# A recurrent branch with its first tap, two squares and small copies on ScalarE, and gelu's polynomial in one VectorE operation

## The chip, the cores and the metric

The kernel runs on one core of a Trainium2 chip. A core has a matmul engine (TensorE, PE in the profile), VectorE (DVE), ScalarE (ACT), GpSimd (POOL) and a sync engine that issues DMAs (SyncE, SP). Each engine works through its own instructions in order; semaphores make one engine wait for another. The metric is device microseconds of the whole program, the median of several runs.

## The reference

One layer of a hybrid decoder for 2048 tokens of width 1024, all in float32:

```python
h = rms_norm(x, g1)
z = h @ w_in                                   # q, k, v, xr, gr
attn = dilated_attention(q, k, v)              # 8 heads, three dilations
xr = causal_depthwise_conv(xr, conv_w, conv_b) # 4 taps in time
r = sigmoid(xr @ w_r + b_r); i = sigmoid(xr @ w_i + b_i)
a = exp(-8 * r * softplus(-lam))
u = sqrt(1 - a * a) * (i * xr)
hid[t] = a[t] * hid[t - 1] + u[t]
rec = hid * gelu(gr)
x = x + rms_norm(concat(attn, rec) @ w_out, g2)
x = x + rms_norm(squared_relu_mlp(rms_norm(x, g3), w1, w2), g4)
```

What the change touches lies between `xr` and `rec`: the recurrent branch.

## The kernel before

The tokens are worked in two halves of 1024, each in two token blocks of 512, and the 512 channels of the recurrent branch in four groups of 128. So the branch consists of 16 blocks of 128 channels by 512 tokens; a block is named half_group_token block, so 1_2_0 is the first token block of group 2 in the second half. `recurrent_block` (L296 to L345) computes one.

Every matrix product with weights is made in three matmuls of a high and a low part: the weights are split on arrival by `split` (L54 on ACT, L55 on POOL or DVE), and `product` (L198 to L200) adds the three up over eight steps of the inner dimension in one PSUM bank.

A block runs as follows. `product` gives the conv input. DVE puts the last three inputs of the token block before it ahead of the new ones (L303, from `tail`), scales the product by the tokens' norm into `xr` (L304), and keeps the new last three (L305). POOL makes the first tap (L307), DVE adds three more (L310), all in `xc`. PE makes the two gates' products from `xc`, `pr` (L313) and `pi` (L315), which outside the kernel's start share a PSUM bank with one buffer. ACT turns them into `r` (L318) and `i` (L320) by tanh, then makes `th` (L323) and, in place of `r`, the factor a by exp (L324). DVE squares a (L326, named `a2`) and takes it into `th` (L327), ACT takes the root (L328), DVE multiplies (L329, L330), runs the recurrence over the 512 tokens (L331, the scan) into `xc`, and keeps its last value in `state` (L332). A second product goes through DVE as `gr` (L335); its gelu is a polynomial on POOL (L338 to L340), a tanh on ACT (L341) and two DVE steps (L342, L343). The block is then written to DRAM by a DMA that POOL issues (L345).

`xr`, `r`, `i`, `th`, `a2`, `gr` and `ge` have one buffer each, so a block's tile waits for the last reader of the block before it. The functions of ACT come in tables; a change of table is a row ACT_TABLE_LOAD.

The blocks are strung together with the attention: `ORDER` (L1557) interleaves the first half's recurrent groups (r02, r03), its products of q, k, v and two attention parts; `BETWEEN` holds the four groups of the second half; groups 0 and 1 of the first half come before both. Up to about 600 us the order on each engine is the scheduler's: it plays the program through a timeline of its own (`schedule_with_timeline_sim`) and issues each instruction where that timeline has it ready. So a change of an instruction's engine moves others. From the out-projection on, the order of the rest is fixed elsewhere.

`cst["pool"]` is an instruction behind which POOL issues copies of w_out and w2 to DRAM scratch (L1459), eight DMAs behind each group of the second half.

## Time and profile before

| | us |
|---|---|
| median of three runs | 2313.2 (2310.83 to 2317.4) |
| the profiled execution | 2311.64 |
| its span in the trace | 2309.9 |

| engine | busy us | share of the span |
|---|---|---|
| PE | 2184.8 | 95% |
| DVE | 1539.9 | 67% |
| ACT | 1231.3 | 53% |
| POOL | 465.9 | 20% |

Of the chain of work that ended last, PE is 59%, DVE 14%, DMA 9% and ACT 7%. The shares are means over a program whose stages differ: in the first 600 us attention, the recurrent branch and the input products share the engines, and from there on the out-projection and the MLP run. What a step of the recurrent branch costs must be read where it runs, as the idle time of PE in front of an instruction and as the clock PE is granted there (1.00 stands for full speed).

### The profile page before, as it was taken

Reading aid. Unit: us, or ns where it says so; the run is one execution under the profiler, and the core shown is the slowest. Engines: PE = TensorE matmul, PEld = TensorE weight load, DVE = VectorE, ACT = ScalarE, POOL = GpSimd, SP = SyncE. Lnnn points to the kernel's source line nnn. Section 1 sums busy time; section 2 is a strip of 40 time slices with the busy share of each in tenths; the row PEclk is TensorE's granted clock in tenths of the full one; section 3 lists DMA queues with packets and bytes.
Section 4 is the critical chain, followed back from the end, with each engine's and each line's share of the span. In section 5 each row is a group of like instructions: output and inputs, shape, how many; then the busy total and the mean of one; then the engine's idle time right before and its main releaser. Section 6 shows DMA issues by size and latency. Waiting matters only on the chain.

```text
span 2309.9 us, 30833 instructions
## 1 busy us (share of the span) xinstructions
PE 2184.8 (95%) x10264; PEld 1776.1 (77%) x10264; DVE 1539.9 (67%) x3060; ACT 1231.3 (53%) x2489; POOL 465.9 (20%) x549
## 2 busy tenths in 40 slices
PE   8989989889999899998999999889999999999998
PEld 6668778667788677786777787667878888788887
DVE  6757575887548877674667677767775656545556
ACT  7646464645334555453656666745454545563542
POOL 5543514563213201011001011113200000000003
PEclk9999999999999999999999999999999999999999
DMA  8364574645754586867777777768454433576665
GB/s 288 99 194 154 166 232 146 180 144 151 255 166 155 195 306 255 302 232 268 248 201 211 220 227 204 220 189 257 147 194 169 164 137 155 208 271 195 192 192 182
DMA packets 217553, 466.16 MB, mean 202 GB/s; under 512 B 22465, under 2 KB 77153, under 8 KB 211121
## 3 DMA queue, kind: packets, MB, share of 16 engines
q1 hardware_dynamic: 188624, 329.52, 45.7%
q0 software_dynamic: 28768, 134.66, 16.5%
q8 instruction: 81, 1.33, 0.2%
q14 instruction: 80, 0.65, 0.1%
HBM read 329.75 MB, written 151.13 MB: 208 GB/s over the span
## 4 chain that ended last, share of the span: by engine, by line
PE 59%; DVE 14%; DMA 9%; ACT 7%; issue 5%; POOL 1%; SPq 0%; DVEq 0%; ACTq 0%; POOLq 0%
PE o L1141 6%; PE o L1140 6%; PE o L1142 6%; PE za L1001 4%; PE za L1002 4%; PE za L1003 4%; PE z L198 3%; PE z L199 3%; PE z L200 3%; PE m L827 2%; PE m L825 2%; PE m L826 2%; PE zc L1001 2%; PE zc L1002 2%; PE zc L1003 2%
## 5 line engine op out<-in xcount | busy, mean ns | idle before, releaser
L198 PE MATMUL z<-hH,wH 128*128 128x512 f32 x640 | 263.6, 412 | 17.6 <-ACT wH L54 7.9
L199 PE MATMUL z<-hL,wH 128*128 128x512 f32 x640 | 259.1, 405 | 0.5 <-DVE hL L173 0.5
L200 PE MATMUL z<-hH,wL 128*128 128x512 f32 x640 | 257.9, 404 | 0.0
L198 PEld LDWEIGHTS z<-hH,wH 128*128 128x128 f32 x640 | 122.6, 192 | 51.2 <-ACT wH L54 8.8
L199 PEld LDWEIGHTS z<-hL,wH 128*128 128x128 f32 x640 | 122.3, 191 | 32.0 <-issue 5.1
L200 PEld LDWEIGHTS z<-hH,wL 128*128 128x128 f32 x640 | 122.5, 191 | 28.5 <-issue 3.4
L415 ACT ACTIVATE smB<-smB,negB 128x128 f32<-128x128 f32 (+3 forms) x128 | 71.4, 559 | 103.0 <-DVE negB L411 102.7
L55 POOL TENSOR_TENSOR wL<-wraw,wH 128x512 fp32r<-128x512 f32 x58 | 84.2, 1464 | 115.7 <-ACT wH L54 109.0
L1006 ACT ACTIVATE sq<-sq 128x512 f32<-128x512 f32 x93 | 58.8, 632 | 84.9 <-DVE sq L1010 84.9
L1066 POOL DMA_DIRECT2D sa<-sq x31 | 16.5, 533 | 402.4 <-ACT sq L1007 401.8
L415 ACT ACTIVATE sm<-sm,neg 128x256 f32<-128x256 f32 (+1 forms) x128 | 63.1, 494 | 55.7 <-DVE neg L411 55.2
L55 DVE TENSOR_TENSOR tlB<-pT_B,thB 128x384 fp32r<-128x384 f32 x96 | 57.4, 598 | 44.2 <-ACT thB L54 41.0
L1007 ACT ACTIVATE sq<-sq 128x512 f32<-128x512 f32 x124 | 76.6, 629 | 2.2
L54 ACT CAST wH<-wraw 128x512 fp32r<-128x512 f32 (+1 forms) x81 | 47.2, 612 | 49.5 <-PE z L199 31.7
L1174 POOL TENSOR_TENSOR y<-y,g4b 128x512 f32<-128x512 f32 x8 | 13.0, 1655 | 261.3 <-ACT junk_y L84 261.3
L1077 DVE TENSOR_TENSOR w2s<-w2s 128x512 f32<-128x512 f32 x64 | 44.1, 689 | 32.1 <-DMA w2s<-in_dram 31.2
L404 DVE CUSTOM_DVE_ANT_0 smB<-SB,mask_b 128x128 f32<-128x128 f32 (+3 forms) x128 | 59.5, 482 | 6.8 <-PE pT_B L377 4.2
L377 PE MATMUL pT_B<-ident,smB 128*128 128x128 f32 x320 | 52.7, 280 | 5.3 <-DVE nb L398 2.2
L54 ACT CAST thB<-pT_B 128x384 fp32r<-128x384 f32 x96 | 48.4, 506 | 16.3 <-PE oB L612 14.2
L55 DVE TENSOR_TENSOR tlA<-pT,thA 128x512 fp32r<-128x512 f32 (+1 forms) x64 | 42.5, 668 | 21.0 <-ACT thA L54 20.7
L1001 PE MATMUL za<-hHT,f_6H 128*128 128x512 f32 x128 | 50.6, 396 | 5.2 <-ACT sq L1040 5.1
L1002 PE MATMUL za<-hLT,f_5H 128*128 128x512 f32 x128 | 51.0, 399 | 4.4 <-DVE hLT L55 4.4
(568 smaller groups left out, 7105.7 us busy)
## 6 DMA issues: line engine op xcount, KB each, us to landing
sa<-as POOLq DMA_DIRECT2D x32, 1024.0 KB, 6.5
w1r<-in_dram SPq DMA_DIRECT2D x58, 512.0 KB, 3.8
sa<-sq POOLq DMA_DIRECT2D x31, 768.0 KB, 3.9
wraw<-in_dram SPq DMA_DIRECT2D x79, 256.0 KB, 3.5
w2s<-in_dram SPq DMA_DIRECT2D x16, 1024.0 KB, 7.5
sb<-w2s POOLq DMA_DIRECT2D x16, 1024.0 KB, 6.2
kh<-sk SPq DMA_DIRECT2D x24, 512.0 KB, 5.2
kl<-sk SPq DMA_DIRECT2D x24, 512.0 KB, 6.8
```

The costliest lines, as they stand in the source:

```text
L54: return (nc.scalar.copy(out=hi, in_=src), (lo_eng or nc.vector).tensor_tensor(out=lo, in0=src, in1=f32(hi), op=ALU.subtract))
L55: (lo_eng or nc.vector).tensor_tensor(out=lo, in0=src, in1=f32(hi), op=ALU.subtract))
L198: pe.matmul(z, hi[:, k, :], hh, start=(k == 0), stop=False)
L199: pe.matmul(z, hi[:, k, :], hl, start=False, stop=False)
L200: pe.matmul(z, lo[:, k, :], hh, start=False, stop=(k == KT - 1))
L415: s.activation(out=sm[:, c0:c0 + w], in_=sm[:, c0:c0 + w], func=AF.Exp, bias=neg[:, j:j + 1], accum_out=st[:, 1, u, cols[j]:cols[j] + 1])
L1001: pe.matmul(o, hi[:, k], bh[:, k], start=start and k == 0, stop=False, skip_group_check=True)
L1002: pe.matmul(o, hi[:, k], bl[:, k], start=False, stop=False, skip_group_check=True)
L1003: pe.matmul(o, lo[:, k], bh[:, k], start=False, stop=k == KH - 1, skip_group_check=True)
L1140: pe.matmul(o, ah[:, ts], bh, start=fresh and j == 0, stop=False, skip_group_check=True)
L1141: pe.matmul(o, ah[:, ts], bl, start=False, stop=False, skip_group_check=True)
L1142: pe.matmul(o, al[:, ts], bh, start=False, stop=j == NJ - 1, skip_group_check=True)
```

## The change

Four edits in `recurrent_block`, and one that follows from them:

- the two small copies (L303, L305) go from DVE to ACT;
- the first tap goes from POOL to ACT, as an activation with the tap's weight as scale and the bias as bias;
- a's square goes from DVE to ACT;
- gelu's square goes from POOL to ACT, and the two POOL steps behind it become one DVE step, (gr²+1/0.044715)·gr; the constant 0.044715 moves into the scale of the tanh;
- since the first tap is no longer on POOL, `cst["pool"]` becomes POOL's last weight split in `load_w`.

```diff
--- before.py
+++ after.py
@@ -108,7 +108,9 @@
             k0 = half * (KT // 2)
             raw = (px or self.pa).tile([P, KT // 2, P], F32, tag="wraw", bufs=6 if px else 2, name=f"wraw{hf}_{ct}_{half}")
             nc.sync.dma_start(out=raw, in_=self.w_in[ct, :, k0:k0 + KT // 2, :])
-            split(nc, hi[:, k0:k0 + KT // 2, :], lo[:, k0:k0 + KT // 2, :], raw, lo_eng=lo_eng or self.lo)
+            made = split(nc, hi[:, k0:k0 + KT // 2, :], lo[:, k0:k0 + KT // 2, :], raw, lo_eng=lo_eng or self.lo)
+            if not px and self.lo is nc.gpsimd:
+                self.cst["pool"] = made[1]
         return hi, lo
 
     def load_start(self, ct, px):
@@ -295,17 +297,16 @@
 
     def recurrent_block(self, hf, c, b, wx, wg, px):
         nc, p, vec = self.nc, px if px and c % 2 else self.pl, self.vec
-        v, s, g, pe = nc.vector, nc.scalar, nc.gpsimd, nc.tensor
+        v, s, pe = nc.vector, nc.scalar, nc.tensor
         n = f"{hf}_{c}_{b}"
         t0 = hf * HT + b * TB
         zx = self.product(hf, 12 + c, wx, b, "B" if px else "P")
         xr = p.tile([P, TB + 3], F32, tag="xr", bufs=1, name=f"xr{n}")
-        v.tensor_copy(out=xr[:, 0:3], in_=self.tail[:, c, :])
+        s.copy(out=xr[:, 0:3], in_=self.tail[:, c, :])
         v.tensor_tensor(out=in_time(xr[:, 3:TB + 3]), in0=by_residue(zx), in1=by_residue(self.bc[b]), op=ALU.mult)
-        v.tensor_copy(out=self.tail[:, c, :], in_=xr[:, TB:TB + 3])
+        s.copy(out=self.tail[:, c, :], in_=xr[:, TB:TB + 3])
         xc = p.tile([P, TB], F32, tag="xc", bufs=2 if p is self.pl else 1, name=f"xc{n}")
-        self.cst["pool"] = g.tensor_scalar(out=xc, in0=xr[:, 3:TB + 3], scalar1=self.cw[:, c, 3:4],
-                                           scalar2=vec["cb"][:, c:c + 1], op0=ALU.mult, op1=ALU.add)
+        s.activation(out=xc, in_=xr[:, 3:TB + 3], func=AF.Identity, scale=self.cw[:, c, 3:4], bias=vec["cb"][:, c:c + 1])
         for t in (2, 1, 0):
             v.scalar_tensor_tensor(out=xc, in0=xr[:, t:t + TB], scalar=self.cw[:, c, t:t + 1], in1=xc,
                                    op0=ALU.mult, op1=ALU.add)
@@ -323,7 +324,7 @@
         s.activation(out=th, in_=r, func=AF.Tanh, scale=self.pcs[:, c:c + 1], bias=self.pcs[:, c:c + 1])
         s.activation(out=r, in_=r, func=AF.Exp, scale=self.ncs[:, c:c + 1], bias=self.ncs[:, c:c + 1])
         a2 = p.tile([P, TB], F32, tag="la", bufs=1, name=f"a2{n}")
-        v.tensor_tensor(out=a2, in0=r, in1=r, op=ALU.mult)
+        s.activation(out=a2, in_=r, func=AF.Square)
         v.scalar_tensor_tensor(out=th, in0=a2, scalar=1.0, in1=th, op0=ALU.add, op1=ALU.mult)
         s.activation(out=th, in_=th, func=AF.Sqrt, scale=0.25)
         v.scalar_tensor_tensor(out=i, in0=i, scalar=1.0, in1=xc, op0=ALU.add, op1=ALU.mult)
@@ -335,10 +336,9 @@
         v.tensor_tensor(out=gr, in0=zg, in1=self.bc[b], op=ALU.mult)
 
         ge = p.tile([P, TB], F32, tag="ge", bufs=1, name=f"ge{n}")
-        g.tensor_tensor(out=ge, in0=gr, in1=gr, op=ALU.mult)
-        g.tensor_scalar(out=ge, in0=ge, scalar1=0.044715, scalar2=1.0, op0=ALU.mult, op1=ALU.add)
-        g.tensor_tensor(out=ge, in0=ge, in1=gr, op=ALU.mult)
-        s.activation(out=ge, in_=ge, func=AF.Tanh, scale=SQ2PI)
+        s.activation(out=ge, in_=gr, func=AF.Square)
+        v.scalar_tensor_tensor(out=ge, in0=ge, scalar=1.0 / 0.044715, in1=gr, op0=ALU.add, op1=ALU.mult)
+        s.activation(out=ge, in_=ge, func=AF.Tanh, scale=SQ2PI * 0.044715)
         v.scalar_tensor_tensor(out=ge, in0=ge, scalar=1.0, in1=gr, op0=ALU.add, op1=ALU.mult)
         v.scalar_tensor_tensor(out=by_residue(ge), in0=by_residue(ge), scalar=0.5, in1=in_time(xc), op0=ALU.mult,
                                op1=ALU.mult)
```

Lines of the new kernel stand a little lower: L303 becomes L305, L304 L306, L305 L307, the first tap L309, the taps L311, `pr` L314, `pi` L316, `r` L319, `i` L321, `th` L324, a by exp L325, a's square L327, its use L328, the root L329, L329 to L332 become L330 to L333, `gr` L336, gelu's square L339, its polynomial L340; L341 to L345 keep their numbers, and L198 to L200 become L200 to L202.

The order on PE before, around `pr` and `pi` of block 1_2_1, with products of z1_15_0 (conv input of block 1_3_0) at both sides:

```order
L199 MATMUL z1_15_0_5289<-hL2_3_3314,wH1_15_5269 128x512
L200 MATMUL z1_15_0_5289<-hH2_3_3313,wL1_15_5270 128x512
L198 MATMUL z1_15_0_5289<-hH2_4_3319,wH1_15_5269 128x512
L199 MATMUL z1_15_0_5289<-hL2_4_3320,wH1_15_5269 128x512
L313 MATMUL pr1_2_1_5207<-xc1_2_1_5202,bd_r_232 128x512
L315 MATMUL pi1_2_1_5209<-xc1_2_1_5202,bd_i_236 128x512
L200 MATMUL z1_15_0_5289<-hH2_4_3319,wL1_15_5270 128x512
L198 MATMUL z1_15_0_5289<-hH2_5_3325,wH1_15_5269 128x512
```

`pi` follows `pr` at once and writes the same bank.

On PE now, the rows around the same `pr`, with attention's output (oB) ahead of it:

```order
L612 MATMUL oB0_6_0_4303<-tlB0_4321,vb0_6_4170 128x256
L612 MATMUL oB0_6_0_4303<-thB0_4320,vb0_6_4170 128x128
L612 MATMUL oB0_6_0_4303<-tlB0_4321,vb0_6_4170 128x128
L314 MATMUL pr1_2_1_5194<-xc1_2_1_5189,bd_r_232 128x512
L202 MATMUL z1_15_0_5275<-hH2_5_3317,wL1_15_5256 128x512
L200 MATMUL z1_15_0_5275<-hH2_6_3323,wH1_15_5255 128x512
L201 MATMUL z1_15_0_5275<-hL2_6_3324,wH1_15_5255 128x512
```

`pr` is followed by the products of z1_15_0, and `pi` comes 30 rows later.

On PE now, the rows around `pi` of that block, with attention (oB, the transposed scores pT) ahead and a product of group 3's gate (z1_19_0) behind:

```order
L612 MATMUL oB0_6_2_4355<-thB0_4372,vb0_6_4170 128x128
L612 MATMUL oB0_6_2_4355<-tlB0_4373,vb0_6_4170 128x128
L377 MATMUL pT0_0_7_0_1_4430<-ident_60,sm0_7_2_4419 128x128 x2
L316 MATMUL pi1_2_1_5196<-xc1_2_1_5189,bd_i_236 128x512
L202 MATMUL z1_19_0_5328<-hH2_3_3305,wL1_19_5266 128x512
L200 MATMUL z1_19_0_5328<-hH2_4_3311,wH1_19_5265 128x512
```

`pr` and `pi` stood back to back; now 29 rows of PE stand between them.

The order on ACT before, in the same place, from r of block 1_2_0 to r of 1_2_1:

```order
L318 ACTIVATE r1_2_0_5123<-pr1_2_0_5119,vec_br_226 128x512
L323 ACTIVATE th1_2_0_5127<-r1_2_0_5123,pcs_271 128x512
L324 ACTIVATE r1_2_0_5123<-r1_2_0_5123,ncs_270 128x512
L328 ACT_TABLE_LOAD
L328 ACTIVATE th1_2_0_5127<-th1_2_0_5127 128x512
L54 CAST wH1_19_5279<-wraw1_19_0_5281 128x512
L320 ACT_TABLE_LOAD
L320 ACTIVATE i1_2_0_5125<-pi1_2_0_5121,vec_bi_228 128x512
L318 ACTIVATE r1_2_1_5211<-pr1_2_1_5207,vec_br_226 128x512
```

Between r and i there are th, the exponential, the root with its table and a weight cast.

On ACT now, from the casts behind r of block 1_2_0 to its i:

```order
L54 CAST wH1_15_5255<-wraw1_15_1_5261 128x512
L339 ACTIVATE ge1_2_0_5153<-gr1_2_0_5151 128x512
L325 ACTIVATE r1_2_0_5111<-r1_2_0_5111,ncs_270 128x512
L307 COPY tail_276<-xr1_2_1_5185 128x3
L309 ACTIVATE xc1_2_1_5189<-xr1_2_1_5185,vec_cb_224,cw_222 128x512
L327 ACTIVATE a21_2_0_5118<-r1_2_0_5111 128x512
L341 ACTIVATE ge1_2_0_5153<-ge1_2_0_5153 128x512
L397 COPY fold_4280<-oA0_6_1_4269 64x512
L329 ACT_TABLE_LOAD
L329 ACTIVATE th1_2_0_5115<-th1_2_0_5115 128x512
L321 ACT_TABLE_LOAD
L321 ACTIVATE i1_2_0_5113<-pi1_2_0_5109,vec_bi_228 128x512
```

The gelu's square, the tail copy, the next block's first tap and a's square now stand between r and i of 1_2_0.

On POOL, between the two halves of the weight split of group 15 (L55), stood the first tap of block 1_2_1 and eight of the DMA issues of L1459. Now the two halves stand together, and the DMA issues of L1459 stand in groups of eight behind whole splits.

## Rows read from the trace of the kernel before

**Rows 1.** Table of windows, two stretches, its first line names the columns.
```profile
core 0: us, PE busy (x) PEld busy (x) DVE busy (x) ACT busy (x) POOL busy (x), PEclk, DMA share, GB/s
...
95.00:175.00 80.00, 69.55 (x281) 53.27 (x280) 46.19 (x64) 30.14 (x48) 38.32 (x35) 0.94 0.62 184
...
430.00:560.00 130.00, 112.02 (x521) 85.54 (x520) 114.36 (x205) 75.91 (x144) 70.01 (x73) 0.93 0.48 149
```

**Rows 2.** Timeline of PE: start, us, instruction, [idle before <-what ended it].
```profile
100.37 1.78 PE L313 MATMUL pr<-xc,bd_r 128*128 128x512 f32 x2 [3.41 <-DVE xc L310]
...
136.54 1.12 PE L313 MATMUL pr<-xc,bd_r 128*128 128x512 f32 x2 [3.21 <-ACT i L320]
...
156.97 0.80 PE L198 MATMUL z<-hH,wH 128*128 128x512 f32 x1 [3.84 <-DVE state L332]
...
458.95 0.58 PE L553 MATMUL oA<-thA,va 128*128 128x256 f32 x1 [5.47 <-DVE state L332]
...
487.88 0.50 PE L198 MATMUL z<-hH,wH 128*128 128x512 f32 x1 [1.72 <-DVE gr L335]
...
503.47 2.07 PE L315 MATMUL pi<-xc,bd_i 128*128 128x512 f32 x2 [4.82 <-ACT r L318]
...
544.97 2.07 PE L315 MATMUL pi<-xc,bd_i 128*128 128x512 f32 x2 [2.88 <-ACT r L318]
```

**Rows 3.** Groups by line, 0 to 660 us: busy, mean ns | idle before, releaser.
```profile
L307 POOL TENSOR_SCALAR xc<-xr,cw,vec_cb 128x512 f32<-128x512 f32 x16 | 13.6, 851 | 32.9 <-DVE xr L304 32.5 <-DVE negB L411 0.2
...
L338 POOL TENSOR_TENSOR ge<-gr 128x512 f32<-128x512 f32 x16 | 19.3, 1205 | 24.5 <-DVE gr L335 17.1 <-DMA smix<-ge 7.3
...
L339 POOL TENSOR_SCALAR ge<-ge 128x512 f32<-128x512 f32 x16 | 13.4, 835 | 1.5
...
L340 POOL TENSOR_TENSOR ge<-ge,gr 128x512 f32<-128x512 f32 x16 | 23.3, 1453 | 1.0
...
L55 POOL TENSOR_TENSOR wL<-wraw,wH 128x512 fp32r<-128x512 f32 x58 | 84.2, 1464 | 115.7 <-ACT wH L54 109.0 <-PE z L200 6.3
...
L303 DVE COPY xr<-tail 128x3 f32<-128x3 f32 x16 | 6.5, 412 | 0.2
...
L305 DVE COPY tail<-xr 128x3 f32<-128x3 f32 x16 | 8.2, 511 | 0.1
...
L326 DVE TENSOR_TENSOR a<-r 128x512 f32<-128x512 f32 x16 | 15.1, 943 | 12.4 <-ACT r L324 12.3
```

**Rows 4.** Timeline of DVE, then of POOL, near 500 us.
```profile
488.87 2.54 DVE L305 COPY tail<-xr 128x3 f32<-128x3 f32 x1
...
497.48 2.76 DVE L329 SCALAR_TENSOR_TENSOR i<-i,xc 128x512 f32<-128x512 f32 x1
...
510.75 0.15 DVE L305 COPY tail<-xr 128x3 f32<-128x3 f32 x1
...
491.35 4.20 POOL L1459 DMA_DIRECT2D sw<-in_dram  x8
...
497.41 1.05 POOL L338 TENSOR_TENSOR ge<-gr 128x512 f32<-128x512 f32 x1
...
498.42 1.25 POOL L55 TENSOR_TENSOR wL<-wraw,wH 128x512 fp32r<-128x512 f32 x1
...
508.11 1.73 POOL L340 TENSOR_TENSOR ge<-ge,gr 128x512 f32<-128x512 f32 x1
```

**Rows 5.** Groups that price the added operations, 0 to 660 us and whole span (L1007).
```profile
L342 DVE SCALAR_TENSOR_TENSOR ge<-ge,gr 128x512 f32<-128x512 f32 x16 | 14.1, 884 | 7.8 <-ACT ge L341 7.6
...
L323 ACT ACTIVATE th<-r,pcs 128x512 f32<-128x512 f32 x16 | 13.0, 814 | 0.3
...
L328 ACT ACT_TABLE_LOAD x16 | 20.5, 1283 | 0.3
...
L1382 ACT ACTIVATE eps<-eps 128x1 f32<-128x1 f32 x1 | 0.2, 203 | 0.0
...
L1007 ACT ACTIVATE sq<-sq 128x512 f32<-128x512 f32 x124 | 76.6, 629 | 2.2
```

## The prediction

> **What bounds the kernel now.** I read the table of windows first. In it, look at how much of each stretch the matmul engine (PE) is busy and at the clock it is granted. From 430 to 560 us, where the eight recurrent blocks of the second half run (one of them ends before it), PE is busy for 112.02 of 130 us at a mean clock of 0.93, VectorE (DVE) for 114.36, GpSimd (POOL) for 70.01 and ScalarE (ACT) for 75.91. From 95 to 175 us, where some of the first half's eight blocks run, PE is busy for 69.55 of 80 us at 0.94 [rows 1]. PE is the bound of the kernel as a whole, so this branch costs time only where PE waits for it; what it costs DVE, ACT or POOL elsewhere is hidden.
>
> Next I read PE's timeline there, for the bracket that tells how long PE stood before an instruction and what it waited for [rows 2]. Seven waits over 1.5 us are this branch's: 3.41, 3.21 and 3.84 in the first stretch, which is 10.5 us, and 5.47, 1.72, 4.82 and 2.88 in the second, which is 14.9 us. Together they are 25.4 us. Four end on DVE (a tap, two state copies, gr) and three on ACT (the gate tanhs of r and i).
>
> After such a wait PE runs at a lower clock for a while. The windows give that loss as (1−0.94)×80 = 4.8 and (1−0.93)×130 = 9.1 us [rows 1]. Part of this low clock is granted while PE stands idle, and there it costs nothing; I count four fifths, 3.8 and 7.3, by my own choice. So the most that a perfect recurrent branch could give back is 10.5+3.8 = 14.3 us in the first stretch and 14.9+7.3 = **22.2 us** in the second, 36.5 in all. After 660 us the work is not touched, and PE's order there is that of before.
>
> **What is removed and moved.** On POOL each block loses the first tap and three gelu steps: 0.851+1.205+0.835+1.453 = 4.34 us by the means of [rows 3], which is 69.5 us over 16 blocks, and 34.8 of the 70.0 us that POOL is busy in the second stretch. POOL is never what PE waits for in [rows 2], so this gives nothing by itself. What it can give is DVE's speed. The same three-column copy takes 2.54 us at 488.87 while POOL works and issues DMAs, and 0.15 us at 510.75, after POOL's last operation has ended (508.11+1.73 = 509.84). A 128x512 step takes 2.76 at 497.48 beside POOL's square (L338) and its weight splits (L55) [rows 4], where L342, the same kind of operation, has a mean of 0.884 [rows 5]. Some of what lies beside DVE there goes (L338), and some stays (L55, 58 splits of 1.464 us each, 84.2 us in all, and the 4.20 us of DMA issues).
>
> The Trainium skill, "SBUF — State Buffer", section "Who interferes with whom", says that DVE and GpSimd share a pair of ports as an exclusive lock, which would explain rows such as 497.48. By that rule alone the two engines' common time shrinks with POOL's work, and half of POOL's work in the second stretch goes; the time would be the first rival's, 2280.
>
> DVE itself loses the head copy (0.412), the tail copy (0.511) and a's square (0.943), 1.87 us per block, and gains one polynomial step, priced at 0.884 by the like step L342: 0.98 us less per block, 7.9 us over the eight of the second stretch, where DVE is busy 88% and is the engine that PE's longest wait (5.47) is for [rows 1 to 3, 5].
>
> **What is added.** ACT gets, per block, the first tap at 0.814 (price of L323, an ACT operation of the same size with two pointer operands), two squares at 0.629 (L1007) and two small copies. These have no row of their own on ACT; a 128x1 operation takes 0.203 and a full square 0.629, and I take 0.2, since 128x3 is nearer to 128x1. That is 2.47 us per block, 39.6 in all, or up to 53 at the upper end. The order also holds 52 table loads instead of 50 on ACT, 2×1.28 = 2.6 us [rows 5], which I count as hidden. In the second stretch ACT goes from 75.9 to about 95.7 of 130 us (74%), so most of the added work fits into time that ACT has free. What does not fit is what stands directly ahead of a gate tanh. The order shows this: ahead of th and i of block 1_2_0 there now stand the gelu's square, the next block's tail copy, its first tap and a's square (0.63+0.2+0.81+0.63 = 2.3 us), and of these only a's square belongs to that chain. So I charge the three PE waits that end on ACT with 2 us each, **6 us**; the bounds are 0 (hidden) and twice that.
>
> Each POOL or DVE step replaced on a chain has a near equal price: the first tap 0.851 against 0.814, a's square 0.943 against 0.629. The gelu chain gets shorter (3.49 against 0.629+0.884 = 1.51), but in [rows 2] only the wait of 1.72 on gr is near it. I cost these at nothing; the cover is that the scan, not the gelu, ends each block.
>
> The Trainium skill, "ScalarE: Activation LUTs", section "Rules for kernel authors", says to do multiplications on VectorE and not on ScalarE. Here the row speaks against it: a's square is 0.943 on DVE and a square is 0.629 on ACT [rows 3, 5]. By the page the squares would be a loss on ACT, the charge above would be at its upper bound of 12 and the time 2303; by the rows a's square gains 0.3 us per block, and the sum holds neither.
>
> The anchor of the copies of w_out and w2 to DRAM moves from the first tap to the last weight split on POOL. A group of eight issues (4.20 us on POOL, [rows 4]) stood between the two halves of the split of group 15; now such a group follows a whole split and delays none of its halves. The DMA engines are busy for 0.48 of the second stretch [rows 1] and what these issues copy is w2, which only the MLP reads, so I cost the move at nothing.
>
> **The sum.** PE's order is the clearest sign in the second stretch. Before, pr and pi of block 1_2_1 stand back to back in one bank, and pi must wait until r has read pr; r in turn waits for its one buffer, which block 1_2_0 holds until its scan has read it: the wait of 4.82. Now some thirty rows of products and attention stand between the two, so that wait has cover. The 5.47 and the 2.88 hang on the same DVE chain, which loses work and some neighbours. I take two thirds of 22.2, **14.8 us**. In the first stretch no such distance shows, and two of its waits are a DVE chain that loses 0.98 us per block and the POOL steps beside it; the third is i on ACT, which gains work. I take half of 14.3, **7.1 us**. Together −14.8 −7.1 +6 = −15.9. Against the profiled execution (2311.6 us, its span 2309.9) that is 2295.7; this run lies 1.6 us under the median of the three, 2313.2, and from the median I get **2297 us**.
>
> **The rivals.**
> All of it comes back. If POOL's removed work is what stretches DVE, the whole 36.5 us return, and ACT's 6 us are hidden or half so: 2313.2−36.5+3 = 2280. For it: half of POOL's busy time goes in the stretch with most waits. Against it: the splits and DMA issues that stay stretch DVE too [rows 4], and one wait (3.21) is for ACT. The port rule of the Trainium skill, named above, is the case for this one. Chance 0.14.
>
> Nothing measurable comes back. The splits keep DVE slow, a third of the prize returns (12.2 us), and the ACT queue takes twice my charge (12 us): 2313. For it: the splits have more time on POOL (84.2 us) than any of the removed steps; the order in the whole of 0 to 600 us is dealt anew, and waits may only change their place. Against it: the thirty or so rows now between pr and pi. The copies and steps do move as the change says, so that it does nothing is only this case. Chance 0.19.
>
> Slower: ACT's queue becomes the bound. ACT runs in order. The small copies and the tap wait for DVE's xr, and everything behind them waits too: weight casts, on which PE waits elsewhere, softmax exponentials and the gates. If each of the eight blocks of the second stretch gets one new PE wait of the added 2.47 us, that is 19.8 us, and with the clock at 11.1/25.4 = 0.44 us per us of wait 28.5; with a third of the prize returned, 2313.2+28.5−12.2 = 2329. It decides against the change from (12.2+6.9)/(2.47×1.44) = 5.4 blocks on. For it: three waits already end on ACT. Against it: ACT has a quarter of the stretch free. Chance 0.12.
>
> **How the numbers follow.** The forecast's own case, 2297, has 0.55, with its own range from 2283 (ACT costs nothing, five sixths return) to 2306 (two fifths return, ACT costs 8). Rounds of this kernel cannot tell less than about 0.3%, 6.9 us, from no change; 2306.3 is the border. Faster: 0.55+0.14 = 0.69; same 0.19; slower 0.12. For 8 in 10 the range runs from 2281, which leaves about 0.1 of the first rival outside, to 2314, which leaves out the last and a little of the second.
>
> **What would show it.** Right: in 430 to 560 us PE's idle time falls from 18 us to about 6 and its clock rises to 0.97; the 4.82 before pi of 1_2_1 is gone; the small copies are all near 0.2 us on ACT; DVE's gelu step (L342) has a mean below 0.80. The rival on ACT would show as PE waits that end on r, i or wH of 2 us and more; the rival of no change as DVE rows over 2 us beside L55 on POOL. I am wrong if the new order puts PE behind a wait that [rows 2] does not have.

## The result and the profile after

The changed kernel takes 2300.76 us (median of seven runs, 2295.1 to 2306.26) against 2313.2 us for the kernel before (seven runs too, 2310.83 to 2323.35). The medians differ by 12.4 us, or 0.5%. The ratio on record, which is not the quotient of the two medians, is 0.9927, or 0.7% faster, with a 95% interval from 0.9905 to 0.9949. The forecast was 2297 with a range from 2281 to 2314. The time lies in the range and the sign is right. The reasons held only in part, and the runs below show which.

The profiled execution took 2302.81 us, with a span of 2300.9. First the windows of the changed kernel (columns as in [rows 1]), then the three windows of the kernel before that stand in no group ahead of the prediction:

```profile
0.00:95.00 95.00, 84.37 (x340) 64.40 (x340) 54.14 (x109) 75.32 (x124) 28.79 (x51) 1.00 0.62 203
95.00:175.00 80.00, 70.49 (x288) 54.63 (x289) 42.67 (x53) 38.79 (x58) 27.61 (x24) 0.96 0.62 188
175.00:430.00 255.00, 245.15 (x1392) 204.93 (x1391) 179.16 (x482) 161.97 (x407) 83.11 (x79) 0.99 0.65 197
430.00:560.00 130.00, 119.30 (x566) 92.96 (x566) 98.53 (x190) 84.97 (x169) 38.01 (x44) 0.99 0.40 128
560.00:660.00 100.00, 97.32 (x433) 78.52 (x432) 43.78 (x80) 32.90 (x64) 19.20 (x15) 1.00 0.71 227
```

Of the kernel before:

```profile
0.00:95.00 95.00, 85.84 (x350) 65.42 (x351) 67.35 (x121) 70.42 (x108) 50.88 (x65) 1.00 0.63 204
...
175.00:430.00 255.00, 241.48 (x1326) 200.67 (x1325) 167.82 (x452) 143.66 (x361) 93.41 (x87) 0.98 0.60 179
...
560.00:660.00 100.00, 98.63 (x465) 80.28 (x464) 49.50 (x81) 32.03 (x60) 15.86 (x13) 1.00 0.67 206
```

In 430 to 560 us PE's idle time falls from 18.0 us to 10.7 and the clock rises from 0.93 to 0.99; DVE's busy time falls from 114.4 to 98.5 and POOL's from 70.0 to 38.0. In 95 to 175 us little changes.

The front part of the kernel ends where the out-projection begins, since from there on PE's order is the same in both, matmul for matmul in the two traces. That is the first start of L825, the first time behind the comma (the columns are the shortest, median and longest duration in ns, then the first and last start in us). I call it the **marker**. Of the kernel before:

```profile
L825 PE MATMUL m<-woH,m_0H x128: 387/389/628, 650.8 to 1674.9; 128*128 128x512 f32 x128
```

And of the changed kernel:

```profile
L825 PE MATMUL m<-woH,m_0H x128: 387/389/776, 633.3 to 1665.1; 128*128 128x512 f32 x128
```

The front part became 17.5 us shorter. From the marker to the end of the span the changed kernel took 2300.9−633.3 = 1667.6 us and the kernel before 2309.9−650.8 = 1659.1, so 8.5 us of the 17.5 are missing at the end of these two executions.

PE's waits of 1 us and more in the two stretches of [rows 2], in the changed kernel:

```profile
98.03 0.50 PE L200 MATMUL z<-hH,wH 128*128 128x512 f32 x1 [3.50 <-DVE zn L230]
...
103.73 1.10 PE L314 MATMUL pr<-xc,bd_r 128*128 128x512 f32 x2 [2.42 <-DVE xc L311]
...
155.99 0.79 PE L200 MATMUL z<-hH,wH 128*128 128x512 f32 x1 [3.88 <-DVE zn L227]
...
455.23 0.77 PE L200 MATMUL z<-hH,wH 128*128 128x512 f32 x1 [4.09 <-DVE gr L336]
...
461.09 0.33 PE L377 MATMUL pT_B<-ident,smB 128*128 128x128 f32 x1 [1.43 <-ACT smB L415]
...
473.59 1.12 PE L314 MATMUL pr<-xc,bd_r 128*128 128x512 f32 x2 [1.02 <-ACT i L321]
...
490.18 1.12 PE L314 MATMUL pr<-xc,bd_r 128*128 128x512 f32 x2 [1.23 <-ACT i L321]
...
496.48 0.91 PE L377 MATMUL pT<-ident,sm 128*128 128x128 f32 x5 [1.04 <-DVE tlB L55]
```

In the first stretch there are 9.8 us of such waits where [rows 2] has 10.5: they have changed their place and are not gone. In the second stretch 5.47, 1.72, 4.82 and 2.88 (and one of 1.26) became 4.09 and four of 1.0 to 1.4.

The groups of the changed kernel that answer to [rows 3] and [rows 5] (busy, mean ns):

```profile
L311 DVE SCALAR_TENSOR_TENSOR xc<-xr,cw,xc 128x512 f32<-128x512 f32 x48 | 38.1, 796 | 5.2 <-ACT xc L309 4.9
...
L328 DVE SCALAR_TENSOR_TENSOR th<-a,th 128x512 f32<-128x512 f32 x16 | 11.6, 728 | 6.8 <-ACT a L327 6.7
...
L342 DVE SCALAR_TENSOR_TENSOR ge<-ge,gr 128x512 f32<-128x512 f32 x16 | 12.0, 747 | 7.5 <-ACT ge L341 7.4
...
L309 ACT ACTIVATE xc<-xr,vec_cb,cw 128x512 f32<-128x512 f32 x16 | 13.0, 815 | 0.0
L327 ACT ACTIVATE a<-r 128x512 f32<-128x512 f32 x16 | 10.0, 624 | 0.1
L307 ACT COPY tail<-xr 128x3 f32<-128x3 f32 x16 | 3.0, 189 | 12.7 <-DVE xr L306 12.7
```

The added ACT operations cost what was priced: 0.815, 0.624 and 0.189 us against 0.814, 0.629 and 0.2. DVE's steps beside POOL became shorter: L342 0.747 (0.884 before, [rows 5]), the taps 0.796 and the use of a's square 0.728, where the kernel before has these rows:

```profile
L310 DVE SCALAR_TENSOR_TENSOR xc<-xr,cw,xc 128x512 f32<-128x512 f32 x48 | 51.1, 1066 | 4.1 <-POOL xc L307 3.4
...
L327 DVE SCALAR_TENSOR_TENSOR th<-a,th 128x512 f32<-128x512 f32 x16 | 17.1, 1066 | 0.2
```

### The profile page after: what moved, and what is told of

Its sections match the earlier page's. It is cut to its first block, busy times and chain, and to the rows that moved or that the text cites. A ratio compares the mean times of both kernels' runs of the same rounds, so it can differ in the third digit from the quotient of the medians.

```text
span 2300.9 us, 30842 instructions
## 1 busy us (share of the span) xinstructions
PE 2182.3 (95%) x10264; PEld 1777.4 (77%) x10264; DVE 1503.5 (65%) x3028; ACT 1267.0 (55%) x2571; POOL 388.5 (17%) x485
## 3 DMA queue, kind: packets, MB, share of 16 engines
q0 software_dynamic: 28768, 134.66, 16.5%
## 4 chain that ended last, share of the span: by engine, by line
PE 49%; DVE 9%; DMA 8%; ACT 6%; issue 4%; POOL 1%; SPq 0%; DVEq 0%; ACTq 0%; POOLq 0%
PE o L1141 6%; PE o L1140 6%; PE o L1142 6%; PE za L1001 4%; PE za L1002 4%; PE za L1003 4%; PE zc L1001 2%; PE zc L1002 2%; PE zc L1003 2%; PE m L825 2%; PE m L826 2%; PE m L827 2%; PE zb L1001 1%; PE zb L1002 1%; PE zb L1003 1%
## 5 line engine op out<-in xcount | busy, mean ns | idle before, releaser
L200 PE MATMUL z<-hH,wH 128*128 128x512 f32 x640 | 259.2, 405 | 20.5 <-DVE zn L227 5.2
L202 PE MATMUL z<-hH,wL 128*128 128x512 f32 x640 | 259.7, 407 | 0.0
L200 PEld LDWEIGHTS z<-hH,wH 128*128 128x128 f32 x640 | 122.0, 191 | 52.9 <-issue 10.1
L202 PEld LDWEIGHTS z<-hH,wL 128*128 128x128 f32 x640 | 121.9, 190 | 29.1 <-issue 4.8
L1006 ACT ACTIVATE sq<-sq 128x512 f32<-128x512 f32 x93 | 58.8, 633 | 90.3 <-DVE sq L1010 90.3
L55 POOL TENSOR_TENSOR wL<-wraw,wH 128x512 fp32r<-128x512 f32 x58 | 80.1, 1396 | 129.4 <-ACT wH L54 120.0
L55 DVE TENSOR_TENSOR tlB<-pT_B,thB 128x384 fp32r<-128x384 f32 x96 | 57.3, 598 | 41.3 <-ACT thB L54 40.5
L1066 POOL DMA_DIRECT2D sa<-sq x31 | 16.5, 533 | 399.6 <-ACT sq L1007 399.0
L1007 ACT ACTIVATE sq<-sq 128x512 f32<-128x512 f32 x124 | 76.7, 629 | 2.3
L55 DVE TENSOR_TENSOR tlA<-pT,thA 128x512 fp32r<-128x512 f32 (+1 forms) x64 | 42.6, 670 | 22.2 <-ACT thA L54 21.9
L404 DVE CUSTOM_DVE_ANT_0 sm<-S,mask_a 128x256 f32<-128x256 f32 (+1 forms) x128 | 47.6, 409 | 10.2 <-PE S L529 8.1
```

Of the source, the lines that this page charges most:

```text
L55: (lo_eng or nc.vector).tensor_tensor(out=lo, in0=src, in1=f32(hi), op=ALU.subtract))
L200: pe.matmul(z, hi[:, k, :], hh, start=(k == 0), stop=False)
L202: pe.matmul(z, lo[:, k, :], hh, start=False, stop=(k == KT - 1))
L404: v.tensor_tensor_reduce(out=sm[:, c0:c0 + w], in0=sp[:, c0:c0 + w], in1=mask[:, mask.shape[-1] - w:], scale=1.0, scalar=-3.0e38, op0=ALU. ...
```

## The experiments

The question was which part of the change gives the 17.5 us. Four theories were held against each other. **A**: POOL's work beside DVE was the price, because it stretches DVE's operations. **B**: DVE's own load was the price. **C**: since the scheduler deals the order of all engines anew at every edit of this part, the gain is the draw and not the work moved. In the traces PE's order in front of the marker first differs from that of before at the 147th of 2892 matmuls in the changed kernel, and at the 475th in null_anchor2, which moves no work. **D**, formed later: one place of the old order was the price, the two gate matmuls that stood next to each other.

All results in one table. The marker is from one profiled execution of each, and that execution can lie off the kernel's median (2301.63 us in only_copies and 2322.05 in pi_late, for medians of 2310.08 and 2317.09); only the kernel before has two, 2.1 us apart. So differences of a few us between markers carry little. The ratio is against runs of the kernel before on the same chip, whose medians in these sets lay between 2312.55 and 2316.42 us.

| kernel | what it is | marker us | median us | ratio, 95% interval |
|---|---|---|---|---|
| before | | 650.8, 648.7 | 2313.2 | |
| changed | all edits | 633.3 | 2300.76 | 0.9927, 0.9905 to 0.9949 |
| only_gelu | before + gelu | 631.5 | 2302.94 | 0.9945, 0.9927 to 0.9963 |
| only_tap | before + first tap + its anchor | 634.3 | 2303.39 | 0.9944, 0.9922 to 0.9965 |
| only_a2 | before + square of a | 640.9 | 2313.5 | 0.9996, 0.9975 to 1.0017 |
| only_copies | before + small copies | 637.7 | 2310.08 | 0.9974, 0.9955 to 0.9994 |
| null_anchor | before, anchor on the last split | 641.1 | 2311.81 | 0.9981, 0.9964 to 0.9998 |
| null_anchor2 | before, anchor on gelu's third step | 630.9 | 2294.16 | 0.9917, 0.9893 to 0.9942 |
| null_anchor3 | before, anchor on the block's DMA | 642.2 | 2309.68 | 0.9971, 0.9955 to 0.9987 |
| after_anchor3 | changed, anchor on the block's DMA | 636.3 | 2304.33 | 0.9944, 0.9922 to 0.9965 |
| pi_late | before, second gate matmul of two blocks held back, with what follows it | 647.2 | 2317.09 | 1.0012, 0.9996 to 1.0027 |
| dead_pool | changed, gelu steps on POOL as dead work | 683.2 | 2354.32 | 1.0179, 1.0151 to 1.0207 |
| tap_and_gelu | before + first tap + gelu | 618.6 | 2295.16 | 0.9919, 0.9900 to 0.9938 |

### The four parts alone

Each is the kernel before with one part of the diff; of the code only added lines are shown, and `...` marks what is left out:

```diff
+        s.activation(out=ge, in_=gr, func=AF.Square)
+        v.scalar_tensor_tensor(out=ge, in0=ge, scalar=1.0 / 0.044715, in1=gr, op0=ALU.add, op1=ALU.mult)
+        s.activation(out=ge, in_=ge, func=AF.Tanh, scale=SQ2PI * 0.044715)
```

> The kernel before with the gelu edit alone (square on ScalarE, polynomial in one VectorE step). In the changed kernel the first out-projection matmul starts at 633.3 us, before at 650.8, so the front part gained 17.5 us. Theory A (GpSimd's work beside VectorE was the price): this edit takes 56.0 of the 69.5 us that GpSimd loses, so the front marker comes to 635 to 640 us and the median to 2299 to 2304. Theory B (VectorE's own load was the price): VectorE gains 13.6 us of work, so the marker stays at 650 to 656 and the median at 2312 to 2318. Theory C (the whole order is dealt anew and the gain is not any part's): a shift of a few us in either direction.

```diff
+                self.cst["pool"] = made[1]
...
+        s.activation(out=xc, in_=xr[:, 3:TB + 3], func=AF.Identity, scale=self.cw[:, c, 3:4], bias=vec["cb"][:, c:c + 1])
```

> The kernel before with the first tap on ScalarE alone, and the anchor of the copies moved with it. Theory A: GpSimd loses 13.6 of 69.5 us, marker 646 to 649 us, median 2309 to 2311. Theory B: VectorE's load does not change, marker 650 to 652, median 2313. Theory C: a few us in either direction.

```diff
+        s.activation(out=a2, in_=r, func=AF.Square)
```

> The kernel before with the square of a on ScalarE alone. Theory A: GpSimd is not touched, marker 650 to 652 us, median 2313. Theory B: VectorE loses 15.1 us of work of the net 16 it loses in all, so the marker comes to 640 to 645 and the median to 2302 to 2307. Theory C: a few us in either direction.

```diff
+        s.copy(out=xr[:, 0:3], in_=self.tail[:, c, :])
...
+        s.copy(out=self.tail[:, c, :], in_=xr[:, TB:TB + 3])
```

> The kernel before with the two small copies on ScalarE alone. Theory A: GpSimd is not touched, marker 650 to 652 us, median 2313. Theory B: VectorE loses 14.7 us of work, so the marker comes to 640 to 645 and the median to 2302 to 2307. Theory C: a few us in either direction.

The markers came 19.3, 16.5, 9.9 and 13.1 us earlier. That is 58.8 us in all, where the whole change has 17.5. In time the gelu and the tap gain 0.5 to 0.6%, the copies 0.3%, and the square nothing (0.9996, 0.9975 to 1.0017). A holds for the gelu (whose marker is earlier still than it expected), but not for the tap (16.5 against 2 to 5 expected) nor, at the marker, for the square and the copies, which leave POOL alone. B holds for these two at the marker only (its medians were 2302 to 2307, measured are 2313.5 and 2310.08), and it fails for the gelu, which adds work to DVE. C had expected a few us in either direction. Four shifts of 10 to 19 us, all in one direction, fit it only if the order of before was a slow one of many. From here on C stands for that, and it needed an edit that moves no work.

### The order alone

Three kernels keep every operation on its engine and only put the anchor elsewhere, behind which POOL issues the copies to DRAM. The first is a part of the change itself. In the other two the first tap is no longer the anchor either.

```diff
-        self.cst["pool"] = g.tensor_scalar(out=xc, in0=xr[:, 3:TB + 3], scalar1=self.cw[:, c, 3:4],
+        g.tensor_scalar(out=xc, in0=xr[:, 3:TB + 3], scalar1=self.cw[:, c, 3:4],
...
+                self.cst["pool"] = made[1]
```

> The kernel before with every operation on the engine where it was; only the anchor of the copies moves from the first tap to GpSimd's last weight split, as in the change. That moves DMA issues on GpSimd and, through the scheduler, the order on all engines. The four parts alone brought the start of the out-projection (650.8 us before) to 631.5, 634.3, 640.9 and 637.7 us, gains of 19.3, 16.5, 9.9 and 13.1 that add up to 58.8 where the whole change has 17.5. Theory C (the order of before was a slow one of many, and every edit deals a new one): marker 632 to 645 us although no work has moved, median 2300 to 2312. Theory A (GpSimd's work beside VectorE): marker 649 to 652, median 2313 to 2316.

```diff
-        g.tensor_tensor(out=ge, in0=ge, in1=gr, op=ALU.mult)
+        self.cst["pool"] = g.tensor_tensor(out=ge, in0=ge, in1=gr, op=ALU.mult)
```

> The kernel before with every operation on the engine where it was; the anchor of the copies is the third gelu step on GpSimd instead of the first tap. A second way to deal the order anew with no work moved. Theory C: marker 632 to 645 us. Theory A: 649 to 652.

```diff
-        nc.gpsimd.dma_start(out=scr_cols(self.scr["mix"][hf][4 + c], b), in_=ge)
+        self.cst["pool"] = nc.gpsimd.dma_start(out=scr_cols(self.scr["mix"][hf][4 + c], b), in_=ge)
```

> The kernel before with every operation on its engine and the anchor of the copies on the DMA issue that ends a block (L345). A third order with no work moved; the two others had markers 641.1 and 630.9. Theory C (any new order is faster than that of before): marker 630 to 642, median 2293 to 2312. The gates of 1_1_1 and 1_2_1 stand 27 and 40 rows apart here.

All three are faster, as C expected: markers 9.7, 19.9 and 8.6 us earlier than 650.8, and ratios whose whole intervals lie below one. (The second and the third marker lie 1.1 and 0.2 us outside the ranges stated.) The second is as fast as the change (0.9917 and 0.9927, with intervals that overlap), although no operation has left its engine. Its DVE steps are still stretched, as these groups of null_anchor2 show (0 to 660 us, busy and mean ns):

```profile
L310 DVE SCALAR_TENSOR_TENSOR xc<-xr,cw,xc 128x512 f32<-128x512 f32 x48 | 47.5, 991 | 4.3 <-POOL xc L307 3.9
...
L327 DVE SCALAR_TENSOR_TENSOR th<-a,th 128x512 f32<-128x512 f32 x16 | 15.5, 967 | 0.2
L342 DVE SCALAR_TENSOR_TENSOR ge<-ge,gr 128x512 f32<-128x512 f32 x16 | 14.2, 889 | 5.5 <-ACT ge L341 5.5
```

A tap takes 0.991 us there, 0.796 in the changed kernel and 1.066 before; L342 takes 0.889, and 0.884 before. Yet PE waits less, as the window of null_anchor2 shows:

```profile
430.00:560.00 130.00, 122.33 (x584) 94.43 (x581) 110.65 (x203) 74.82 (x142) 71.31 (x77) 0.99 0.49 154
```

PE is idle for 7.7 of 130 us, with DVE busy for 110.7 and POOL for 71.3. Another kernel agrees: only_tap, with its marker 16.5 us earlier and a ratio of 0.9944, has taps as long as before:

```profile
L311 DVE SCALAR_TENSOR_TENSOR xc<-xr,cw,xc 128x512 f32<-128x512 f32 x48 | 51.2, 1072 | 3.5 <-ACT xc L309 3.1
```

So shorter DVE steps are not needed for the gain; another order alone does as well.

Two limits belong to this. It is not the old anchor alone that was slow, since only_gelu, only_a2 and only_copies keep it on the first tap and have markers 9.9 to 19.3 us earlier. And the three kernels are not wholly empty edits: they also change when POOL issues the copies, eight of which take 4.20 us of POOL [rows 4]. The DMA engines' share in the second stretch is 0.49 in null_anchor2 and 0.48 before; beyond that the runs do not part the new place of the copies from the new order.

### What the moved work is worth beside the order

The changed kernel with the anchor of null_anchor3:

```diff
-                self.cst["pool"] = made[1]
...
+        self.cst["pool"] = nc.gpsimd.dma_start(out=scr_cols(self.scr["mix"][hf][4 + c], b), in_=ge)
```

> The changed kernel with its anchor on the same DMA issue (L345) as null_anchor3, so that the two differ by the moved operations alone and by what the scheduler makes of them. If the moved operations are worth something at all, this is faster than null_anchor3 by 5 us or more at the marker, as the changed kernel is against null_anchor (633.3 against 641.1, the same anchor). If the gain is the order alone, the two lie within the spread of orders, 10 us either way: 625 to 645.

With the same anchor, the moved work brings the marker from 642.2 to 636.3 (5.9 us) and the median from 2309.68 to 2304.33, in one set of runs on one chip. Eight of the ten runs of after_anchor3 took 2305.7 us or less, and one of the ten of null_anchor3. At the change's own anchor the marker goes from 641.1 to 633.3 (7.8 us) and the ratio, in two sets of runs, from 0.9981 to 0.9927, with intervals that do not overlap. Both pairs point the same way, by 0.27 and 0.54%, or 6 to 12 us. But the intervals of the first pair overlap (0.9955 to 0.9987 and 0.9922 to 0.9965), its marker of 636.3 fits both cases of the expectation, and each member of a pair still has an order of its own, so a part of this can be the draw too.

The last run put the two parts together that take work off POOL, only_tap and only_gelu:

```diff
+        s.activation(out=xc, in_=xr[:, 3:TB + 3], func=AF.Identity, scale=self.cw[:, c, 3:4], bias=vec["cb"][:, c:c + 1])
...
+        s.activation(out=ge, in_=gr, func=AF.Square)
+        v.scalar_tensor_tensor(out=ge, in0=ge, scalar=1.0 / 0.044715, in1=gr, op0=ALU.add, op1=ALU.mult)
+        s.activation(out=ge, in_=ge, func=AF.Tanh, scale=SQ2PI * 0.044715)
```

> The kernel before with the two edits that take work off GpSimd (first tap, with its anchor, and gelu), without the copies and the square of a. Alone, each of the two had a ratio of 0.9944 and 0.9945 and a marker of 634.3 and 631.5 us. If their gains are their own and add up, this has 0.989, some 2291 us, and a marker near 615 to 620. If each had mostly its draw of the order, this is one more draw: 0.992 to 0.998, 2298 to 2311 us, marker 630 to 642, as with the four parts, which did not add up either.

Its marker is 618.6, 32.2 us earlier, close to the sum of the two parts (19.3+16.5 = 35.8): at the marker these two add up, and the front part ends 12.3 us before that of the fastest kernel without moved work (630.9). It is still one draw. The time is 2295.16 us (ratio 0.9919) and not 2291 (0.989): in the profiled execution the rest of the kernel took 2292.7−618.6 = 1674.1 us, 6.5 us more than in the changed kernel. One place of that is in the MLP, on ACT (start, us, instruction, idle before and what ended it), in tap_and_gelu:

```profile
869.76 0.58 ACT L1040 COPY sq<-za 128x512 f32<-128x512 f32 x1 [5.03 <-DMA sb<-w2s]
```

PE then starts again at 870.40 after 6.09 us:

```profile
870.40 0.79 PE L1001 MATMUL za<-hHT,f_6H 128*128 128x512 f32 x1 [6.09 <-ACT sq L1040]
```

In the changed kernel the same ACT copy waits for the same transfer too, but less:

```profile
881.16 0.59 ACT L1040 COPY sq<-za 128x512 f32<-128x512 f32 x1 [0.79 <-DMA sb<-w2s]
```

That the earlier front part is the reason is not shown. In pi_late, whose marker is at 647.2, the same copy waits too:

```profile
895.96 0.58 ACT L1056 COPY sq<-za 128x512 f32<-128x512 f32 x1 [2.87 <-DMA sb<-w2s]
```

And in null_anchor2, whose marker is at 630.9, the copy in that place (at 876.45) waits for no transfer.

### The pair of gate matmuls

> The kernel before with one thing moved: the second gate's matmul of blocks 1_1_1 and 1_2_1 (2 rows and 1 row behind the first gate's matmul in the order of before, 17 or more in every faster kernel except two) is traced behind half of the next group's product; they now stand 23 and 9 rows behind. PE's order is that of before up to row 1859, some 435 us. Theory D (the slow place of the order of before is this pair, whose wait of 4.82 us and the clock after it PE pays): the front marker comes from 650 (650.8 and 648.7 in two executions) to 638 to 643 us, median 2303 to 2309. Theory A (GpSimd beside VectorE) and the rival that many small differences of the order add up: marker 647 to 651, median 2313 to 2317.

```diff
+        late = hf and b and c in (1, 2)
+        zg = self.product(hf, 16 + c, wg, b, "P") if late else None
...
+            self.later.append(lambda at: self.recurrent_rest(*args, at))
...
+        with self.tc.issue_after(at[11].ins) if at else contextlib.nullcontext():
+            pe.matmul(pi, self.bd["i"][:, c, :], xc, start=True, stop=True)
```

The edit is wider than `pi`: in these two blocks it also puts the gate's product (zg) ahead of `pi`, and all that follows `pi` in the block behind half of the next group's product. D falls, as far as an edit of this width tests it. The marker is 647.2, and the time that of before (2317.09, ratio 1.0012). The wait of 4.82 is gone, but hardly more work is done in the stretch (527 matmuls, 521 before). The window of pi_late:

```profile
430.00:560.00 130.00, 113.90 (x527) 86.75 (x527) 112.95 (x206) 77.83 (x151) 68.49 (x73) 0.91 0.45 141
```

And PE's timeline of pi_late, with four of the waits:

```profile
454.48 0.58 PE L569 MATMUL oA<-thA,va 128*128 128x256 f32 x1 [5.42 <-DVE state L348]
...
475.54 0.50 PE L200 MATMUL z<-hH,wH 128*128 128x512 f32 x1 [1.47 <-DVE xr L308]
...
500.55 0.39 PE L628 MATMUL oB<-thB,vb 128*128 128x256 f32 x1 [2.21 <-DVE na L414]
...
546.50 0.79 PE L200 MATMUL z<-hH,wH 128*128 128x512 f32 x1 [2.84 <-DVE zn L227]
```

PE's idle time is 16.1 us (18.0 before), the clock 0.91. The longest wait of before (5.47 on the state copy) is still there with 5.42, the others now end on other DVE results, and DVE is as busy as before (112.95). This speaks for the wait at the pair being where the lateness showed and not where it came from.

### Dead work on POOL

> The changed kernel with the three gelu steps of before put back on GpSimd in the second half's eight blocks as dead work: they read gr as before and write a tile that nobody reads. The chain of the changed kernel stays, GpSimd's work beside VectorE returns (8 x 3.49 = 28 us). Theory A: VectorE's stretched operations return in the second stretch, and the marker goes from 633.3 back to 640 to 646 us, the median from 2301 to 2307 to 2312. Theory C: the order is dealt anew once more, the marker is 628 to 640, the median 2295 to 2306.

```diff
+        if hf:
+            un = self.spare.tile([P, TB], F32, tag="un", bufs=1, name=f"un{n}")
+            g.tensor_tensor(out=un, in0=gr, in1=gr, op=ALU.mult)
+            g.tensor_scalar(out=un, in0=un, scalar1=0.044715, scalar2=1.0, op0=ALU.mult, op1=ALU.add)
+            g.tensor_tensor(out=un, in0=un, in1=gr, op=ALU.mult)
```

Neither A nor C expected 683.2 and 2354.32. The window of dead_pool, with PE idle for 48.3 us and the clock at 0.75:

```profile
430.00:560.00 130.00, 81.68 (x354) 63.49 (x354) 72.67 (x130) 59.83 (x121) 65.81 (x66) 0.75 0.35 111
```

One wait, of 23.90 us, is about half of that idle time; the next is of 8.82 us. From the timelines of PE, DVE and POOL in dead_pool:

```profile
450.53 0.58 PE L558 MATMUL oA<-thA,va 128*128 128x256 f32 x1 [8.82 <-DVE na L403]
...
502.51 0.80 PE L200 MATMUL z<-hH,wH 128*128 128x512 f32 x1 [23.90 <-DVE gr L336]
...
501.76 0.69 DVE L336 TENSOR_TENSOR gr<-z,bc 128x512 f32<-128x512 f32 x1 [19.55 <-POOL un L343]
...
487.09 1.25 POOL L694 TENSOR_TENSOR na<-na,co 128x512 f32<-128x512 f32 x1 [39.17 <-DMA co<-sco]
```

The dead steps read gr, which has one buffer. On POOL they stood in line behind an attention step (na) that waited 39.17 us for a transfer. So gr stayed taken, DVE could not write the next one, and PE waited 23.90 us. What the wait of 8.82 hangs on stays open. How much POOL's work stretches DVE, which the run was made for, it shows in the durations only. The DVE step that is 0.747 in the changed kernel and 0.884 before is 0.886 here:

```profile
L347 DVE SCALAR_TENSOR_TENSOR ge<-ge,gr 128x512 f32<-128x512 f32 x16 | 14.2, 886 | 6.2 <-ACT ge L346 5.9
```

What that costs in time is hidden under the long waits. The run does show a price that work on POOL can have in this kernel: it ties the branch's buffers to whatever POOL waits for ahead of it.

### The kernel before once more

> The kernel before, unchanged, for a second profiled execution. If the order sets the front part, its marker is 650.8 us within 1 us again. The rest after the marker took 1651.7 us of first matmul starts in the first profile, and 1655 to 1663 in the changed kernel and the four parts, which issue the same order there. If that is the execution's luck, the second profile of before takes 1655 to 1663 too; if the early start is given back at waits for transfers, it takes 1651 to 1653.

Its marker is 648.7, 2.1 us off where the expectation allowed 1, and the same waits stand in the same places. Of before_again:

```profile
501.26 2.07 PE L315 MATMUL pi<-xc,bd_i 128*128 128x512 f32 x2 [4.87 <-ACT r L318]
```

By the measure of the expectation (from the marker to the last matmul's start) the rest took 1656.7 us here and 1651.7 in the first execution. So in these two executions of one order the front part differs by 2.1 us and the rest by 5.0. Over all kernels the rest, to the end of the span, lies between 1659.1 and 1674.1 us, and not by the marker: 1663.8 with the latest (683.2), 1661.9 with 630.9, 1673.1 with 647.2, 1674.1 with 618.6. The 8.5 us that were missing in the profiled execution of the change can be of this kind: beside the second execution of before (2312.8−648.7 = 1664.1) only 3.5 us are missing. The medians differ by 12.4 us, between the 17.5 of the markers and the 9.0 of the two spans.

## Why the prediction was right, and where it was not

- **The total: near, and partly by luck.** The sum was −14.8 −7.1 +6 = −15.9 us. By the prediction's own count the profiles give 13.5 us for the second stretch, 0.7 for the first and 5.7 for the time between them, which the sum left out, and nothing of the charge of 6. That is 19.9, near the 17.5 of the marker. Of these, 12.4 are in the medians. Terms that were too large, a charge that was not paid and a stretch that was left out cancel in part.
- **The second stretch, 14.8 us of 22.2: right in size, but not by the reason named.** By the same count as in the prediction PE's idle time there fell by 18.0−10.7 = 7.3 us, and four fifths of the clock's part are 0.8×(0.99−0.93)×130 = 6.2: 13.5 us. The forecast signs (idle about 6, clock 0.97) came out as 10.7 and 0.99. The 4.82 ahead of pi of block 1_2_1 is gone, as said. But the rows between pr and pi, the clearest sign of the forecast, are not shown to be the cause: pi_late has such rows and has lost the 4.82 too, and its stretch is no better (idle 16.1, clock 0.91). And null_anchor2, with no work moved, comes to an idle time of 7.7 and a clock of 0.99.
- **The first stretch, 7.1 us of 14.3: wrong.** Idle 10.5 to 9.5 us and a clock of 0.96 for 0.94 give 1.0+0.8×1.6 = 2.2 us, and 1.5 us of that are lost again ahead of it (PE busy 85.84 to 84.37 up to 95 us). Two of the three waits on the branch became waits on another DVE result of the same size (3.50 and 3.88 on zn); the third is still on a tap (2.42).
- **175 to 430 us: not in the sum at all.** Idle 13.5 to 9.9 us and a clock of 0.99 for 0.98 give 3.7+0.8×2.55 = 5.7 us. Recurrent blocks and attention are mixed there, and the prediction looked only at waits that name the branch.
- **ACT's 6 us: not seen.** PE's waits that end on ACT in these stretches were 3.21, 4.82 and 2.88 and are 1.43, 1.02 and 1.23. ACT has room (84.97 of 130 us busy in the second stretch), as the argument against the slower rival said, and that rival did not happen.
- **The rest after the marker, costed at nothing: too short a view.** PE's order is the same there, but its time is not: it differs by 5 us between two executions of one program, and a transfer can hold it (5.03 in tap_and_gelu).
- **The step that failed most is the one on the anchor.** It was costed at nothing, with the DMA engines' share as the reason. Moved alone it brings the marker 9.7 us forward and the ratio to 0.9981 (null_anchor), and moved elsewhere 19.9 and 0.9917 (null_anchor2). The prediction said that the order is dealt anew and used that only for the rival of no change. The runs show a new order as a cause that can by itself be as large as the whole forecast. Beside it the moved work is worth 6 to 12 us at an equal anchor, which is not wholly free of the draw.
- **DVE beside POOL.** The steps became shorter as forecast (L342 0.747, below the 0.80 named), and null_anchor2 is as fast with steps nearly as long as before (taps 0.991 for 1.066, L342 0.889 for 0.884). The rule of the Trainium skill, "SBUF — State Buffer", section "Who interferes with whom", agrees with the shorter durations. That it decides the time, which was the rival of the whole prize (2280), is not borne out by these runs.
- **ScalarE for squares.** The row of the changed kernel, 0.624 us for a's square on ACT against a mean of 0.943 on DVE [rows 3] and 0.677 at the shortest there, stands against the rule of the Trainium skill, "ScalarE: Activation LUTs", section "Rules for kernel authors", for this shape in float32; the page gives its factor for bf16. Yet only_a2 gives no time (0.9996), so no run shows that either price was on the path.

What stays open: why the order of before is slow, since the pair of gate matmuls does not explain it; and how the 6 to 12 us that the moved work gains at an equal anchor divide between shorter DVE steps, less DVE work and the draw of the order. A test needs one fixed order for all engines with and without the edits, which was not tried. Nor was it tried to repeat tap_and_gelu with the square of a or with the copies, so whether these two cost anything in the changed kernel (618.6 against 633.3 at the marker) is not known.

## What to carry to other kernels

Where a scheduler sets the order of all engines, the first control for an edit is one that moves no work but makes the scheduler run on other input. Here three such kernels moved the time by 0.2, 0.3 and 0.8%, as much as the edits did, and a gain of that size cannot be put down to an edit without them. Two kernels lie a little below the change by their ratios (0.9917 and 0.9919 beside 0.9927), within overlapping intervals: null_anchor2, which costs nothing but a moved anchor, and tap_and_gelu, which leaves the square and the copies where they were.

A wait that a trace names is where the lateness shows. Taking the named wait away (pi_late) left other waits on the same late engine, and the time stayed.

## What the runs showed of the hardware

How far an operation on DVE is stretched while POOL works depends on where its inputs lie. Of the kernel before, with shortest, median and longest duration in ns:

```profile
L335 DVE TENSOR_TENSOR gr<-z,bc x16: 672/680/692, 37.2 to 550.0; 128x512 f32<-128x512 f32 x16
...
L342 DVE SCALAR_TENSOR_TENSOR ge<-ge,gr x16: 670/692/1698, 49.7 to 559.9; 128x512 f32<-128x512 f32 x16
...
L303 DVE COPY xr<-tail x16: 148/166/1901, 1.1 to 518.8; 128x3 f32<-128x3 f32 x16
```

The product of a PSUM bank and one SBUF tile (gr) never exceeds 0.692 us in 16 instances, and in four of them (37.2, 38.7, 63.6 and 526.4 us) POOL computes for more than half of the time. The step with two SBUF tiles reaches 1.698, and a copy of three columns 1.901. The Trainium skill, "SBUF — State Buffer", section "Who interferes with whom", states this: a DVE instruction with at most one SBUF input does not contend outside the two-port modes, one with two does with a GpSimd instruction that reads SBUF, and copies can enter these modes. The trace goes further than that in one place. The instance of 1.698 stands beside DMA issues of POOL, and the record does not say why. Of the kernel before:

```profile
455.02 1.70 DVE L342 SCALAR_TENSOR_TENSOR ge<-ge,gr 128x512 f32<-128x512 f32 x1
...
452.65 4.20 POOL L1459 DMA_DIRECT2D sw<-in_dram  x8
```

On ACT the same small copy stays between 178 and 197 ns. Of the changed kernel:

```profile
L307 ACT COPY tail<-xr x16: 178/193/197, 37.4 to 519.2; 128x3 f32<-128x3 f32 x16
```
